# Eight heads at a step in an RWKV recurrence, and SBUF tiles on 64-byte boundaries

## The chip, the cores and the metric

The kernel runs on one core of one Trainium2 chip. The metric is the device time of one execution in microseconds. Three runs of the kernel before took 2035.17 to 2036.27, median 2035.74.

## The reference, cut to what matters

Two transformer blocks are computed on 512 positions of width 1024, all in float32. The first block mixes three branches (a short convolution, a stick-breaking attention, an RWKV-7 recurrence), then has cross attention and a convolutional feed-forward net (FFN); the second has two attentions (FoX and NSA) and a squared-ReLU MLP. The change is in the recurrence, which has eight heads with a 64x64 state each:

```
def step(state, inp):
    r_t, w_t, k_t, v_t, kk_t, a_t = inp
    sa = einsum("bhvk,bhk->bhv", state, kk_t)
    state = state * w_t - sa x (kk_t * a_t) + v_t x k_t
    return state, einsum("bhvk,bhk->bhv", state, r_t)
out = scan(step, 0, ...)                       # 512 steps
out = ((out - mean) * rsqrt(var + GN_EPS)) * lnx_w + lnx_b
return (out + bonus) * sigmoid(xg) @ g_lora
```

## The kernel before, in words

Every large product is made of three matmuls in the type float32r (high by high, low by high, high by low: lines 161, 162, 163 in `mm3`), with 128x128 weights and, mostly, 512 streamed columns. Weights come from HBM in pieces of 4 KB a partition (`wpiece`): SP issues the load, ScalarE rounds the high part (line 145), VectorE or, while `lpool` is set, GpSimd subtracts the low part (line 146). The pieces rotate through two buffers of a base pool and, in some stages, one or two of an extra pool that `weights` opens (two buffers and one extra in the FFN, two and two in the last MLP). These three lines are called the gemm matmuls below.

The recurrence works on chunks of 64 positions: 8 chunks, in two halves of four. `rwkv_prep1` makes, per chunk and head, the decayed keys and queries (tiles `rkr` with kap and rho, `rKB`) and their products `rAB` (line 869); `rwkv_prep2` inverts the triangular part of `rAB` with many matmuls of 16x16 and 32x32 (lines 924 to 945). `rwkv_scan` then goes from chunk to chunk, in two copies with four heads each (`scan(0)`, `scan(1)`):

- line 992: kap (64 weight columns) against the state, for a pair of heads; line 993: a head's `rAB` against the values `rvu`, on top of it, in PSUM partitions 64 to 127; VectorE copies the sum to `rrhs` (line 995);
- line 998: the inverted block against `rrhs`; VectorE copies it into `rvu` (line 999);
- line 1003: the state's update; line 1009: rho (64 weight columns) against the old state; line 1010: `rAB` against `rvu`, added to it in the bank `o`; VectorE adds the update to the decayed state (lines 988, 1016);
- `turn` transposes the next chunk's values and keys on TensorE (lines 969, 974), and after every second chunk `rwkv_post` normalises 128 positions (line 1034 is its matmul).

float32 matmuls run as two passes, each a row of the trace; transposes as one.

All of this is filler work beside gemm matmuls: `first_mixer` weaves `rwkv_mix` with `fill()` (the projections of the recurrence, the convolution branch, the gates, the attention's queries). The order on each engine is then set when the program is built: a scheduler with a model of the engines places the recurrence's instructions between the gemm matmuls, and at run time each engine keeps to that order and waits where it must.

Of the kernel before, what the change touches and what calls it, by code (L numbers as in the profile page):

```python
# [16 lines left out]
T = 512  # L17
# [53 lines left out]

class Core:


    def __init__(self, tc, ctx, cst):
        self.tc, self.nc, self.ctx = tc, tc.nc, ctx
        nc = self.nc
        self.const = ctx.enter_context(tc.tile_pool(name="const", bufs=1))
        self.xp = ctx.enter_context(tc.tile_pool(name="xn", bufs=1))
# [3 lines left out]
        self.wp = ctx.enter_context(tc.tile_pool(name="w", bufs=2))  # L83
# [663 lines left out]
def rwkv_project(core, pool, tmp, w, xh, xl, P, mid, pieces):  # L747

    nc = core.nc
    kr = pool.tile([128, 2, 4, T], F32, name="rkr")  # L750
    R = {"k": kr[:, 0], "r": kr[:, 1], "kr": kr, "v": pool.tile([128, 4, T], F32, name="rv")}
# [4 lines left out]
    def shift(dst, j, ps):  # L756
        t = tmp.tile([128, T + 1], F32, name="ff", bufs=3)
        nc.gpsimd.memset(t[:, 0:1], 0.0)
        nc.scalar.activation(t[:, 1:T + 1], ps, AF.Identity, scale=P["mu"][:, j:j + 1])
        nc.vector.scalar_tensor_tensor(dst, ps, P["omu"][:, j:j + 1], t[:, 0:T], op0=ALU.mult, op1=ALU.add)  # L760
# [15 lines left out]
def rwkv_prep1(core, pool, tmp, P, hf, wait):  # L776
# [6 lines left out]
    rp, kp = (R[n][:, :, ts] for n in "rk")  # L783
    KR = R["kr"][:, :, :, ts]

# [39 lines left out]
    for j in range(4):  # L825
        nc.scalar.activation(sq[:, j], kp[:, j], AF.Square, scale=col("k_k", j))
# [22 lines left out]
    tt(k2, k2, kp, op=ALU.mult)  # L849
    for j in range(4):  # L850
        nc.vector.scalar_tensor_tensor(kp[:, j], kp[:, j], col("k_k", j), pss[j // 2][:, j % 2 * 256:j % 2 * 256 + 256], op0=ALU.mult, op1=ALU.mult)
    KB = pool.tile([128, 4, 4, 2, CH], F32, name="rKB", bufs=2)
    tt(a, kp, a, op=ALU.mult)
# [3 lines left out]
    tt(ct(kp), ct(kp), E[:, :, :, 0:CH], op=ALU.mult)  # L857
    for j in range(4):
        nc.vector.scalar_tensor_tensor(k2[:, j], rp[:, j], col("r_k", j), k2[:, j], op0=ALU.mult, op1=ALU.mult)
    tt(ct(rp), ct(rp), E[:, :, :, 1:], op=ALU.mult)  # L860
# [3 lines left out]
    for c in range(4):  # L864
        for par in range(2):
            hp = slice(64 * par, 64 * par + 64)
            ps = core.pbank().rearrange("p (j t) -> p j t", j=4)
            for j in range(4):
                mm(ps[:, j], KB[hp, j, c].rearrange("p a t -> p (a t)"), KR[hp, :, j, c * CH:(c + 1) * CH], start=True, stop=True)  # L869
# [81 lines left out]
def rwkv_scan(core, pool, P, hf, g, S, o, y):  # L951
# [5 lines left out]
    js = slice(2 * g, 2 * g + 2)  # L957
    KB, AB, wc, bon = core.half[hf]
    KB, AB, wc, bon = KB[:, js], AB[:, :, :, js], wc[:, js], bon[:, :, 4 * g:4 * g + 4]
    KR = core.R["kr"][:, :, js, hf * 256:hf * 256 + 256]  # L960
    vp = core.R["v"][:, js, hf * 256:hf * 256 + 256]
    vb = None
    heads = [(j, par, slice((2 * j + par) * 64, (2 * j + par) * 64 + 64), slice(64 * par, 64 * par + 64)) for j in range(2) for par in range(2)]
    def turn(c):

        vu = pool.tile([128, 256], F32, name="rvu", bufs=4)
        ps = core.sbank()
        for j in range(2):
            nc.tensor.transpose(ps[0:64, j * 128:j * 128 + 128], vp[:, j, c * CH:c * CH + CH], core.ident)
        nc.scalar.activation(vu[0:64], ps[0:64, 0:256], AF.Copy)  # L970
        kw = pool.tile([128, 2, 128], F32, name="rkw", bufs=2)
        tt(kw, KB[:, :, c].rearrange("p j a t -> p j (a t)"), wc[:, :, c].to_broadcast([128, 2, 128]), op=ALU.mult)
        for j in range(2):
            nc.tensor.transpose(ps[:, 256 + j * 128:384 + j * 128], kw[:, j], core.ident)
        kt = pool.tile([128, 2, 128], F32, name="rkt", bufs=4)
        nc.scalar.activation(kt.rearrange("p j t -> p (j t)"), ps[:, 256:512], AF.Copy)
# [4 lines left out]
    for c in range(4):  # L981
        first = hf == 0 and c == 0
        vu, kt = ahead
        if not first:
            sw = pool.tile([128, 2, 64], F32, name="rsw", bufs=2)
            for par in range(2):
                hp = slice(64 * par, 64 * par + 64)
                tt(sw[hp], S[hp, :, hp], wc[hp, :, c].to_broadcast([64, 2, 64]), op=ALU.mult)
        ps = core.sbank()
# [6 lines left out]
        yield  # L996
        for j, par, h, hp in heads:
            mm(ps[64:128, 256 + h.start:256 + h.stop], AB[64:128, c, par, j, 0:64], rhs[64:128, h], start=True, stop=True)
        nc.vector.tensor_copy(vu[64:128], ps[64:128, 256:512])
        yield  # L1000
        ps = core.sbank()[:, 0:128].rearrange("p (j v) -> p j v", j=2)
        for j, par, h, hp in heads:
            mm(ps[hp, j], kt[:, j, hp], vu[:, h], start=True, stop=True)
        if c % 2 == 0:
            vb = pool.tile([128, 4, 64], F32, name="rvb", bufs=2)
        op = slice(64 * (c % 2), 64 * (c % 2) + 64)
        for j, par, h, hp in heads:
            if not first and par == 0:
                mm(o[op, j * 128:j * 128 + 128], KR[:, 1, j, c * CH:(c + 1) * CH], S[:, j], start=True, stop=False)
            mm(o[op, h], AB[:, c, par, j, 64:128], vu[:, h], start=first, stop=first or par == 1)  # L1010
        for par in range(2):
            hp = slice(64 * par, 64 * par + 64)
            if first:
                nc.vector.tensor_copy(S[hp, :, hp], ps[hp])
            else:
                tt(S[hp, :, hp], ps[hp], sw[hp], op=ALU.add)
        tt(vb[op], vu[0:64].rearrange("p (h v) -> p h v", h=4), bon[:, c].to_broadcast([64, 4, 64]), op=ALU.mult)
        if c < 3:
            ahead = turn(c + 1)
        if c % 2 == 1:  # L1020
            rwkv_post(core, pool, P, hf * 2 + c // 2, g, o, vb, y)
# [3 lines left out]
def rwkv_post(core, pool, P, t, g, ps, vb, y):  # L1025
# [3 lines left out]
    gs = slice(g * 256, g * 256 + 256)  # L1029
    o = pool.tile([128, 4, 64], F32, name="ro", bufs=1)  # L1030
    of = o.rearrange("p h v -> p (h v)")
    nc.scalar.activation(of, ps, AF.Copy)
    gt = core.sbank()[:, 0:256]
    nc.tensor.matmul(gt, core.R["g"][:, t * 128:t * 128 + 128], P["gl"][:, gs], start=True, stop=True)
    st = core.small.tile([128, 4, 1], F32, name="gst")
    nc.vector.tensor_reduce(st.rearrange("p h o -> p (h o)"), o, axis=AX.X, op=ALU.add)
    nc.vector.tensor_scalar(st, st, scalar1=1.0 / 64, scalar2=None, op0=ALU.mult)
    tt(o, o, st.to_broadcast([128, 4, 64]), op=ALU.subtract)
    sq = pool.tile([128, 256], F32, name="rkw", bufs=2).rearrange("p (h v) -> p h v", h=4)
    nc.scalar.activation(sq, o, AF.Square)  # L1040
    vr = core.small.tile([128, 4, 1], F32, name="gvr")
    nc.vector.tensor_reduce(vr.rearrange("p h o -> p (h o)"), sq, axis=AX.X, op=ALU.add)
    nc.gpsimd.tensor_scalar(vr, vr, scalar1=1.0 / 64, scalar2=GN_EPS, op0=ALU.mult, op1=ALU.add)
    rs = core.small.tile([128, 4, 1], F32, name="grs")
    nc.gpsimd.tensor_tensor(rs.rearrange("p h o -> p (h o)"), vr.rearrange("p h o -> p (h o)"), core.mhalf[:, 0:4], op=ALU.pow)
# [744 lines left out]
```

## Time and profile before

| | |
|---|---|
| profiled execution | 2035.63 us, span 2033.7 us |
| median of three runs | 2035.74 us |
| mean granted TensorE clock | 0.983 of full speed |
| TensorE (PE) busy | 1971.8 us, 97%, 10908 matmul rows |
| VectorE / ScalarE / GpSimd busy | 1142.3 / 845.2 / 319.9 us |
| gemm matmuls, recurrence between them | about 110 to 432 us from the span's start |

The page's busy time of PE is a sum of pipelined matmuls, so it can't tell how quickly they follow on each other. That is read from the timeline: the difference between the starts of one row and of a later one, divided by the matmuls between.

### The profile page before, as it was taken

The numbers are of one execution on the slowest core, as the hardware profiler recorded it, in microseconds if no ns is written. First come the engines' busy times: TensorE is split into PE (matmuls) and PEld (weight loads), VectorE is DVE, ScalarE is ACT, GpSimd is POOL, SyncE is SP. The second block draws the span as 40 slices with busy tenths as digits, with TensorE's granted clock in tenths as the row PEclk, the third lists the DMA queues.
The fourth block names the chain that finished last, engine by engine and source line by source line (L and its number), as shares of the span: only waits on it lengthen the run. The fifth ranks groups of instructions, "written<-read, shape, count | busy, mean of one in ns | idle before, by whom it ended". The sixth has DMA issues, their size and how long they took to land.

```text
span 2033.7 us, 28099 instructions
## 1 busy us (share of the span) xinstructions
PE 1971.8 (97%) x10908; PEld 1645.9 (81%) x10908; DVE 1142.3 (56%) x1933; ACT 845.2 (42%) x1478; POOL 319.9 (16%) x375
## 2 busy tenths in 40 slices
PE   6999999999899999999999998999999999999998
PEld 5777777778878888788888887888888878888886
DVE  3458453426877545555364456666789754344343
ACT  4433222225644444344243346557766433232232
POOL 1333123334330100200000003002243120000000
PEclk9999989999999999999999998999999999999999
DMA  5223223233347551322333335543222632333331
GB/s 169 73 68 80 68 71 102 90 118 94 105 135 239 152 162 61 105 83 83 104 96 100 94 93 166 143 126 93 63 68 89 196 114 83 101 96 94 95 102 52
DMA packets 281304, 215.03 MB, mean 106 GB/s; under 512 B 28270, under 2 KB 240900, under 8 KB 281044
## 3 DMA queue, kind: packets, MB, share of 16 engines
q1 hardware_dynamic: 261364, 205.23, 33.5%
q10 hardware_dynamic: 19808, 8.02, 1.6%
q8 instruction: 86, 1.41, 0.3%
q14 instruction: 46, 0.38, 0.1%
HBM read 195.35 MB, written 20.48 MB: 106 GB/s over the span
## 4 chain that ended last, share of the span: by engine, by line
PE 85%; DVE 7%; ACT 3%; issue 2%; DMA 2%; POOL 1%; SPq 1%; ACTq 0%; DVEq 0%; POOLq 0%
PE g L161 16%; PE g L162 16%; PE g L163 16%; PE s L161 9%; PE s L163 9%; PE s L162 9%; PE s L589 1%; PE s L603 1%; PE s L285 1%; PE p L869 1%; DVE sbr L673 1%; PE s L577 1%; PE s L576 1%; DMA wr<-in_ca_wkv_dram 1%; DVE ptl L153 1%
## 5 line engine op out<-in xcount | busy, mean ns | idle before, releaser
L145 ACT ACTIVATE wh<-wr 128x1024 fp32r<-128x1024 f32 x307 | 323.6, 1056 | 602.5 <-PE g L162 193.5
L146 DVE TENSOR_TENSOR wl<-wr,wh 128x1024 fp32r<-128x1024 f32 (+1 forms) x240 | 295.2, 1232 | 422.0 <-ACT wh L145 418.1
L161 PE MATMUL g<-xh,wh 128*128 128x512 f32 (+1 forms) x1168 | 454.0, 390 | 6.2 <-DVE rkr L760 2.4
L162 PE MATMUL g<-xl,wh 128*128 128x512 f32 (+1 forms) x1168 | 451.8, 387 | 2.1 <-DVE xl L153 2.1
L163 PE MATMUL g<-xh,wl 128*128 128x512 f32 (+1 forms) x1168 | 451.3, 387 | 0.0
L161 PEld LDWEIGHTS g<-xh,wh 128*128 128x128 f32 x1168 | 224.4, 193 | 50.4 <-issue 3.6
L162 PEld LDWEIGHTS g<-xl,wh 128*128 128x128 f32 x1168 | 224.7, 193 | 43.5 <-DVE xl L153 2.8
L163 PEld LDWEIGHTS g<-xh,wl 128*128 128x128 f32 x1168 | 224.2, 192 | 43.2 <-issue 1.2
L146 POOL TENSOR_TENSOR wl<-wr,wh 128x1024 fp32r<-128x1024 f32 x67 | 166.1, 2482 | 437.3 <-ACT wh L145 424.8
L161 PE MATMUL s<-wh,ah 128*128 128x512 f32 x324 | 127.1, 393 | 0.0
L163 PE MATMUL s<-wh,al 128*128 128x512 f32 x324 | 127.0, 392 | 0.0
L162 PE MATMUL s<-wl,ah 128*128 128x512 f32 x324 | 126.5, 391 | 0.0
L161 PE MATMUL s<-xh,wh 128*128 128x512 f32 x288 | 112.7, 391 | 0.0
L163 PE MATMUL s<-xh,wl 128*128 128x512 f32 x288 | 112.6, 391 | 0.0
L162 PE MATMUL s<-xl,wh 128*128 128x512 f32 x288 | 112.5, 391 | 0.0
L260 POOL TENSOR_TENSOR ss<-rss 128x1 f32<-128x1 f32 (+1 forms) x20 | 6.5, 327 | 464.4 <-ACT rsq L252 464.4
L1097 POOL TENSOR_SCALAR sy<-sy,rsm,ngate 128x128 f32<-128x128 f32 (+1 forms) x64 | 42.4, 666 | 198.8 <-DVE rsm L1095 182.8
L153 DVE TENSOR_TENSOR ptl<-s,pth 128x256 fp32r<-128x256 f32 (+3 forms) x144 | 66.8, 476 | 11.8 <-ACT pth L152 10.8
L163 PEld LDWEIGHTS s<-wh,al 128*128 128x128 f32 x324 | 60.8, 188 | 13.9
L162 PEld LDWEIGHTS s<-wl,ah 128*128 128x128 f32 x324 | 60.8, 188 | 13.6
L161 PEld LDWEIGHTS s<-wh,ah 128*128 128x128 f32 x324 | 60.8, 188 | 13.1
L1093 ACT ACTIVATE sy<-sy,m 128x128 f32<-128x128 f32 (+1 forms) x96 | 53.6, 559 | 39.1 <-DVE m L1091 36.9
(491 smaller groups left out, 3754.4 us busy)
## 6 DMA issues: line engine op xcount, KB each, us to landing
wr<-in_w_ff_dram SPq DMA_DIRECT2D x64, 512.0 KB
wr<-in_w_comb_dram SPq DMA_DIRECT2D x62, 512.0 KB
wr<-in_ffn_up_dram SPq DMA_DIRECT2D x44, 512.0 KB
wr<-in_w_in_dram SPq DMA_DIRECT2D x36, 512.0 KB
wr<-in_ffn_down_dram SPq DMA_DIRECT2D x22, 512.0 KB
wr<-in_ca_wkv_dram SPq DMA_DIRECT2D x16, 512.0 KB
d_gate<-ff SPq DMA_DIRECT2D x24, 256.0 KB
gi<-d_gate SPq DMA_DIRECT2D x24, 256.0 KB
```

The lines of the kernel that those rows point to most:

```text
L145: self.nc.scalar.activation(h, raw, AF.Copy)
L146: (self.nc.gpsimd if pool or self.lpool else self.nc.vector).tensor_tensor(l, raw, h.bitcast(F32), op=ALU.subtract)
L153: nc.vector.tensor_tensor(l, src, h.bitcast(F32), op=ALU.subtract)
L161: mm(out, lh, rh, start=first, stop=False)
L162: mm(out, lh, rl, start=False, stop=False)
L163: mm(out, ll, rh, start=False, stop=last)
L285: nc.tensor.transpose(ps[:, j * 128:(j + 1) * 128], x[:, j * 128:(j + 1) * 128], self.ident)
L576: mm(s, q[:, qs], kk[0][:, 0:n], start=True, stop=False)
L577: mm(s, q[:, qs], kk[1][:, 0:n], start=False, stop=last)
L589: core.nc.tensor.transpose(ps[:, c], p[:, c], core.ident)
L1093: nc.scalar.activation(y, y, AF.Exp, scale=-1.0, bias=m, accum_out=sm)
L1097: nc.gpsimd.tensor_scalar(y, y, scalar1=rs, scalar2=fac, op0=ALU.mult, op1=ALU.mult)
```

## The change: what it does

1. `rwkv_scan` runs once for all eight heads instead of twice for four. `rkr` is stored chunk by chunk with kap and rho side by side, so that one matmul with 128 weight columns (new line 1019) gives for a pair of heads what lines 992 and 1009 gave; both halves stay in the bank `o`, kap's in partitions 0 to 63, rho's in 64 to 127, and the products of lines 993 and 1010 (now 1021 and 1034) are added on top. The two copies from PSUM (now `halves`) are split between VectorE and ScalarE, 256 columns each. `o` goes to SBUF by ScalarE after every chunk. `rvu`, `rkt`, `rkw`, `rsw` and `rrhs` are twice as wide, with half as many buffers or fewer. `rwkv_post` runs four times on 512 columns instead of eight times on 256, and its result leaves in 4 DMAs instead of 8, still on ScalarE's queue.
2. `Lines` rounds the size of each tile up to 64 bytes a partition (the small ones excepted), and a tile of 32 bytes at the edge of the right-hand side shifts what lies there.

```diff
+class Lines:
+    def tile(self, shape, dtype, name, **kw):
+        n, line = math.prod(shape[1:]), 64 // mybir.dt.size(dtype)
+        if n % line == 0:
+            return self.p.tile(shape, dtype, name=name, **kw)
+        t = self.p.tile([shape[0], n + -n % line], dtype, name=name, **kw)[:, 0:n]
...
+        ctx.enter_context(tc.tile_pool(name="edge", bufs=1, side="right")).tile([128, 8], F32, name="edge")
...
-            yield p
+            yield Lines(p)
...
-    kr = pool.tile([128, 2, 4, T], F32, name="rkr")
+    kr = pool.tile([128, 4, T // CH, 2, CH], F32, name="rkr")
...
+    def halves(dst, src):
+        nc.vector.tensor_copy(dst[:, 0:256], src[:, 0:256])
+        nc.scalar.activation(dst[:, 256:512], src[:, 256:512], AF.Copy)
...
+        ps = core.ps.tile([128, 512], F32, name="o")
         if not first:
...
+            for j in range(4):
+                mm(ps[:, j * 128:j * 128 + 128], KR[:, j, c].rearrange("p a t -> p (a t)"), S[:, j], start=j == 0, stop=False, skip_group_check=True)
+        for n, (j, par, h, hp) in enumerate(heads):
+            mm(ps[0:64, h], AB[0:64, c, par, j, 0:64], vu[0:64, h], start=first and n == 0, stop=n == 7, skip_group_check=True)
...
-            if not first and par == 0:
-                mm(ps[64:128, j * 128:j * 128 + 128], KR[:, 0, j, c * CH:(c + 1) * CH], S[:, j], start=True, stop=False)
-            mm(ps[64:128, h], AB[0:64, c, par, j, 0:64], vu[0:64, h], start=first, stop=first or par == 1)
-        rhs = pool.tile([128, 256], F32, name="rrhs", bufs=2)
-        nc.vector.tensor_copy(rhs[64:128], ps[64:128, 0:256])
+        rhs = pool.tile([128, 512], F32, name="rrhs")
+        halves(rhs[64:128], ps[0:64])
...
-            if not first and par == 0:
-                mm(o[op, j * 128:j * 128 + 128], KR[:, 1, j, c * CH:(c + 1) * CH], S[:, j], start=True, stop=False)
-            mm(o[op, h], AB[:, c, par, j, 64:128], vu[:, h], start=first, stop=first or par == 1)
+        for n, (j, par, h, hp) in enumerate(heads):
+            mm(ps[64:128, h], AB[:, c, par, j, 64:128], vu[:, h], start=first and n == 0, stop=n == 7, skip_group_check=True)
...
+        nc.scalar.activation(o[op].rearrange("p h v -> p (h v)"), ps[64:128], AF.Copy)
...
-    return abreast(prep1(), prep2(), scan(0), scan(1))
+    return abreast(prep1(), prep2(), scan())
```

TensorE's order, one chunk step of the recurrence. Before, where both groups of heads come together between gemm matmuls (g<-xh,wh and so on; rS is the state):

```order
L162 MATMUL g<-xl,wh 128x512
L992 MATMUL s<-rS,rkr 64x128
L993 MATMUL s<-rvu,rAB 64x64 x2
L992 MATMUL s<-rS,rkr 64x128
L993 MATMUL s<-rvu,rAB 64x64 x2
L992 MATMUL s<-rS,rkr 64x128
L993 MATMUL s<-rvu,rAB 64x64 x2
L992 MATMUL s<-rS,rkr 64x128
L993 MATMUL s<-rvu,rAB 64x64 x2
L163 MATMUL g<-xh,wl 128x512
```

The same step on TensorE after the change (the gemm lines are now 180 to 182); the next step of the chunk, line 1027, stands 21 gemm matmuls further on, and line 1032 another 19 behind that:

```order
L182 MATMUL g<-xh,wl 128x512
L180 MATMUL g<-xh,wh 128x512
L1019 MATMUL o<-rS,rkr 128x128 x4
L1021 MATMUL o<-rvu,rAB 64x64 x8
L181 MATMUL g<-xl,wh 128x512
```

Four matmuls with 64 weight columns, each between matmuls of another tile shape, have become four with 128 in a row. TensorE at the end of a chunk, after the change (line 1009 is gone from it):

```order
L180 MATMUL g<-xh,wh 128x512
L1032 MATMUL s<-rvu,rkt 64x64 x8
L1034 MATMUL o<-rvu,rAB 64x64 x8
L996 MATMUL s<-ident,rv 64x128 x4
L1002 MATMUL s<-ident,rkw 128x128 x4
L181 MATMUL g<-xl,wh 128x512
```

What stood in two places, one for each four heads, stands in one. In all, the order before has 53 places at which a gemm matmul is followed by one with weights smaller than 128x128, the order after 41, and beyond the recurrence the engines' orders are almost the same.

The tiles' first bytes, as the built programs place them (remainder after division by 256; "pool" is that of the weight pieces):

| tile | before | after |
|---|---|---|
| xh, xl; base pool wh, wl | 32 | 64 |
| extra pool of the FFN | 160 | 128 |
| extra pools of the FoX branch and the last MLP | 224 | 192 |
| fh, fl (FoX branch) | 160 | 192 |
| pth, nv (NSA attention) | 64 | 0 |
| ah, al of the last MLP | 224 | 192 |

While a matmul streams its columns, the weights of the next are loaded. For pairs of 512-column float32r matmuls, the distance between the two starts (first byte of the streamed columns less that of the next weights, modulo 256) is in the two programs:

| distance | 0 | 64 | 128 | 192 | 32 or 224 |
|---|---|---|---|---|---|
| before | 4041 | 1356 | 719 | 28 | 80 |
| after | 4087 | 74 | 1429 | 654 | 0 |

## Rows read from the trace of the kernel before

**Rows 1.** The page, busy time by engine, and the chain that ended last:

```profile
PE 1971.8 (97%) x10908; PEld 1645.9 (81%) x10908; DVE 1142.3 (56%) x1933; ACT 845.2 (42%) x1478; POOL 319.9 (16%) x375
...
PE 85%; DVE 7%; ACT 3%; issue 2%; DMA 2%; POOL 1%; SPq 1%; ACTq 0%; DVEq 0%; POOLq 0%
```

**Rows 2.** Waits of PE, window 100 to 440 us (all of them):

```profile
PE p L924 <- ACT ff L1482: 3.7, 1, 3.7
PE s L992 <- DVE rvu L999: 2.3, 1, 2.3
```

**Rows 3.** Windows: stretch, length, busy of PE, PEld, DVE, ACT, POOL, PEclk:

```profile
275.00:293.00 18.00, 15.71 (x184) 12.41 (x185) 10.91 (x20) 1.94 (x4) 4.34 (x4) 0.53 0.26 75
```

**Rows 4.** Timeline of PE, lines 992 and 993: start, length, instruction, passes:

```profile
340.53 0.39 PE L162 MATMUL g<-xl,wh 128*128 128x512 f32 x1
340.85 0.43 PE L992 MATMUL s<-rS,rkr 128*64 128x128 f32 x2
341.21 0.44 PE L993 MATMUL s<-rvu,rAB 64*64 64x64 f32 x4
...
343.78 0.50 PE L163 MATMUL g<-xh,wl 128*128 128x512 f32 x1
```

**Rows 5.** Timeline of PE, line 1009 between others, and alone:

```profile
356.05 0.39 PE L1009 MATMUL o<-rS,rkr 128*64 128x128 f32 x2
356.27 0.39 PE L1010 MATMUL o<-rvu,rAB 128*64 128x64 f32 x4
...
358.85 0.43 PE L1009 MATMUL o<-rS,rkr 128*64 128x128 f32 x2
359.22 0.44 PE L974 MATMUL s<-ident,rkw 128*128 128x128 f32 x2
```

**Rows 6.** Timeline of PE, float32 passes with 128x128 weights and 128 columns:

```profile
92.08 1.95 PE L843 MATMUL p<-ident,re 128*128 128x128 f32 x16
93.78 0.48 PE L163 MATMUL g<-xh,wl 128*128 128x512 f32 x1
```

**Rows 7.** Timeline of PE in the FFN, first matmuls of three weight pieces:

```profile
881.67 0.39 PE L161 MATMUL g<-xh,wh 128*128 128x512 f32 x1
...
887.11 0.40 PE L161 MATMUL g<-xh,wh 128*128 128x512 f32 x1
...
892.70 0.39 PE L161 MATMUL s<-xh,wh 128*128 128x512 f32 x1
```

**Rows 8.** Timeline of PE, sixteen 64x64 passes in a row:

```profile
348.54 1.14 PE L998 MATMUL s<-rrhs,rAB 64*64 64x64 f32 x16
349.61 0.50 PE L162 MATMUL g<-xl,wh 128*128 128x512 f32 x1
```

**Rows 9.** Timeline of PE in the last MLP, extra-pool pieces, 18 matmuls apart:

```profile
1698.33 0.39 PE L161 MATMUL g<-xh,wh 128*128 128x512 f32 x1
...
1702.45 0.39 PE L161 MATMUL g<-xh,wh 128*128 128x512 f32 x1
```

**Rows 10.** Timeline of PE in the FoX branch, extra-pool pieces, 18 matmuls apart:

```profile
1612.34 0.39 PE L161 MATMUL s<-fh,wh 128*128 128x512 f32 x1
...
1616.54 0.39 PE L161 MATMUL g<-fh,wh 128*128 128x512 f32 x1
```

**Rows 11.** Timeline of PE, line 603 in NSA, then in FoX:

```profile
1413.91 0.28 PE L603 MATMUL s<-pth,nv 128*128 128x256 f32 x1
1414.03 0.28 PE L603 MATMUL s<-ptl,nv 128*128 128x256 f32 x1
...
1605.37 0.28 PE L603 MATMUL s<-ptl,v 128*128 128x256 f32 x1
1605.49 0.28 PE L603 MATMUL s<-pth,v 128*128 128x256 f32 x1
```

**Rows 12.** Groups: VectorE's copy of line 995 (by source), ScalarE's rounding (page):

```profile
L995 DVE COPY rrhs<-s x16: 427/427/428, 132.5 to 416.9; 64x256 f32<-64x256 f32 x16
...
L145 ACT ACTIVATE wh<-wr 128x1024 fp32r<-128x1024 f32 x307 | 323.6, 1056 | 602.5 <-PE g L162 193.5
```

More of the change, by code (lines that the diff above doesn't have):

```diff
@@ L749, in rwkv_project @@
     nc = core.nc
-    kr = pool.tile([128, 2, 4, T], F32, name="rkr")
-    R = {"k": kr[:, 0], "r": kr[:, 1], "kr": kr, "v": pool.tile([128, 4, T], F32, name="rv")}
+    kr = pool.tile([128, 4, T // CH, 2, CH], F32, name="rkr")
+    R = {"k": kr[:, :, :, 0], "r": kr[:, :, :, 1], "kr": kr, "v": pool.tile([128, 4, T], F32, name="rv")}
     R["wa"] = pool.tile([128, T], F32, name="rwa")
@@ L759, in shift @@
         nc.scalar.activation(t[:, 1:T + 1], ps, AF.Identity, scale=P["mu"][:, j:j + 1])
-        nc.vector.scalar_tensor_tensor(dst, ps, P["omu"][:, j:j + 1], t[:, 0:T], op0=ALU.mult, op1=ALU.add)
+        x, y = ps, t[:, 0:T]
+        if len(dst.shape) == 3:
+            x, y = (v.rearrange("p (c t) -> p c t", t=CH) for v in (x, y))
+        nc.vector.scalar_tensor_tensor(dst, x, P["omu"][:, j:j + 1], y, op0=ALU.mult, op1=ALU.add)
     def ev_lora(m, ps):
@@ L782, in rwkv_prep1 @@
     ts = slice(hf * 256, hf * 256 + 256)
-    rp, kp = (R[n][:, :, ts] for n in "rk")
-    KR = R["kr"][:, :, :, ts]
+    rp, kp = (R[n][:, :, hf * 4:hf * 4 + 4] for n in "rk")
+    KR = R["kr"][:, :, hf * 4:hf * 4 + 4]
     def e():
@@ L948, in rwkv_prep2, with rwkv_scan @@
     yield
-def rwkv_scan(core, pool, P, hf, g, S, o, y):
+def rwkv_scan(core, pool, P, hf, S, y):
     nc = core.nc
@@ L999, in rwkv_scan @@
[L999 to L1007, printed above, removed]
-            if not first and par == 0:
-                mm(o[op, j * 128:j * 128 + 128], KR[:, 1, j, c * CH:(c + 1) * CH], S[:, j], start=True, stop=False)
-            mm(o[op, h], AB[:, c, par, j, 64:128], vu[:, h], start=first, stop=first or par == 1)
+            mm(pc[hp, j], kt[:, j, hp], vu[:, h], start=True, stop=True)
@@ L1013, in rwkv_scan @@
             if first:
[L1014 removed]
+                nc.vector.tensor_copy(S[hp, :, hp], pc[hp])
             else:
[L1016 to L1017 removed]
+                tt(S[hp, :, hp], pc[hp], sw[hp], op=ALU.add)
+        op = slice(64 * (c % 2), 64 * (c % 2) + 64)
+        if c % 2 == 0:
+            vb = pool.tile([128, 8, 64], F32, name="rvb")
+            o = pool.tile([128, 8, 64], F32, name="ro")
+        nc.scalar.activation(o[op].rearrange("p h v -> p (h v)"), ps[64:128], AF.Copy)
+        tt(vb[op], vu[0:64].rearrange("p (h v) -> p h v", h=8), bon[:, c].to_broadcast([64, 8, 64]), op=ALU.mult)
         if c < 3:
@@ L1020, in rwkv_scan, with rwkv_post @@
         if c % 2 == 1:
-            rwkv_post(core, pool, P, hf * 2 + c // 2, g, o, vb, y)
+            rwkv_post(core, pool, P, hf * 2 + c // 2, o, vb, y)
         yield
-def rwkv_post(core, pool, P, t, g, ps, vb, y):
+def rwkv_post(core, pool, P, t, o, vb, y):
     nc = core.nc
     tt = nc.vector.tensor_tensor
-    gs = slice(g * 256, g * 256 + 256)
-    o = pool.tile([128, 4, 64], F32, name="ro", bufs=1)
     of = o.rearrange("p h v -> p (h v)")
[L1032 to L1035, printed above, removed]
+    gt = core.sbank()
+    nc.tensor.matmul(gt, core.R["g"][:, t * 128:t * 128 + 128], P["gl"], start=True, stop=True)
+    st = core.small.tile([128, 8, 1], F32, name="gst")
@@ L1036, in rwkv_post @@
     nc.vector.tensor_reduce(st.rearrange("p h o -> p (h o)"), o, axis=AX.X, op=ALU.add)
     nc.vector.tensor_scalar(st, st, scalar1=1.0 / 64, scalar2=None, op0=ALU.mult)
-    tt(o, o, st.to_broadcast([128, 4, 64]), op=ALU.subtract)
-    sq = pool.tile([128, 256], F32, name="rkw", bufs=2).rearrange("p (h v) -> p h v", h=4)
+    tt(o, o, st.to_broadcast([128, 8, 64]), op=ALU.subtract)
+    sq = pool.tile([128, 4, 128], F32, name="rkw").rearrange("p j (a v) -> p (j a) v", a=2)
     nc.scalar.activation(sq, o, AF.Square)
-    vr = core.small.tile([128, 4, 1], F32, name="gvr")
+    vr = core.small.tile([128, 8, 1], F32, name="gvr")
@@ L1059, in rwkv_mix @@
     core.half = {}
-    o = core.ps.tile([128, 512], F32, name="o")
     def wait(u, done):
@@ L1073, in prep2, with scan @@
             yield from rwkv_prep2(core, tmp, P, hf)
-    def scan(g):
+    def scan():
         for hf in range(2):
@@ L1078, in scan @@
             yield from wait("v", core.ready)
-            yield from rwkv_scan(core, pool, P, hf, g, S[:, 2 * g:2 * g + 2], o[:, 256 * g:256 * g + 256], y)
-    return abreast(prep1(), prep2(), scan(0), scan(1))
+            yield from rwkv_scan(core, pool, P, hf, S, y)
+    return abreast(prep1(), prep2(), scan())
 def soft(core, pool, s, bias, fac=None):
```

84 lines of the change are left out of this document (46 added, 38 removed).

## The prediction

> **What bounds the kernel.** I read the page first: busy times, then the chain of waits. TensorE is busy for 97% of the span and holds 85% of the chain; every other engine, weight loads apart, is below 60% [rows 1]. So what counts is the time that TensorE's instructions take one behind the other, and the times at which it has none it may start. The waits of TensorE over the whole stage of the recurrence, 100 to 440 us, come next: there are two, 6.0 us in all [rows 2]. [...] The rest of the stage is the pitch of matmuls, and for that I went to the timeline and subtracted starts. A reader should see that the recurrence's own latency is hidden: its steps stand far apart in TensorE's order, and the gemm matmuls fill the space. A shorter chain of steps is thus worth nothing by itself. What is worth something is fewer or cheaper instructions on TensorE.
>
> **First part: the recurrence on TensorE.** Seven of the eight chunks have a state to multiply. For each of these the first step of both groups takes, from the first pass of line 992 to the next gemm matmul, 343.78 - 340.85 = 2.93 us [rows 4]: eight passes of line 992 and sixteen of line 993. Line 992 alone takes 0.36 us for two passes, because every second one is followed by another tile shape. Line 1009 adds 0.22 us for two passes where it stands between passes of line 1010, 0.37 us where it stands alone [rows 5]; there are four such pairs a chunk, at least 0.88 us. That is 3.81 us a chunk.
>
> In its place come eight passes of line 1019, with 128x128 weights and 128 columns. No row shows that form in this place; the nearest are the sixteen passes of line 843, of the same shapes, at 1.70 us, 0.106 each [rows 6]. So 0.85 us, then a change of tile shape, for which I take what a gemm matmul pays when a smaller one follows, 0.32 instead of 0.23 us [rows 4, 7], so 0.09; then sixteen passes of line 1021 in a row, as line 998 has them: 1.07 us [rows 8]. Sum 2.01 us. **Saved: 1.80 us a chunk, 12.6 us in seven.** From below: if line 1019 keeps line 992's 0.18 us a pass, 2.51 us instead of 2.01, 9.1 us are saved. From above: if all of line 1009's pairs cost 0.37 us, 16.8 us.
>
> The order has 12 places fewer at which a gemm matmul is followed by smaller weights. Each costs 0.09 us going in, and about as much coming out: sixteen passes in 1.07 us hold one exit, and at half the pitch of line 843, 0.053 us, they would take 0.85. I take 0.09 for it too. **Saved: 12 x 0.18 = 2.2 us**, between 0 and that. So the first part is worth 14.8 us, between 9 and 19.
>
> Edits with one answer: transposes keep their number of passes, line 1034 goes from sixteen passes of 256 columns to eight of 512, and the new layout of `rkr` changes no count; nothing. VectorE has 98 instructions fewer, some of them half as long, ScalarE gets 16 copies of 256 columns and 8 of `o`, and its queue issues 4 DMAs fewer: all beside TensorE, which has 19 to 21 gemm matmuls to run between two steps of the chunk. If that cover is gone, each step costs a copy; see the last rival.
>
> **Second part: where tiles begin.** The padding removes no instruction. But in the FFN three pieces of weights follow each other with the same instructions, 24 matmuls each. From 881.67 to 887.11 us, with weights of the base pool, a matmul takes 5.44 / 24 = 0.2267 us; from 887.11 to 892.70, with those of the extra pool, 5.59 / 24 = 0.2329 us [rows 7]. What differs is where the weights begin: in the base pool at the same remainder by 256 as xh, in the extra pool 128 bytes from it. At distance 64 the pitch is 4.12 / 18 = 0.2289 us [rows 9], at 192 it is 4.20 / 18 = 0.2333 [rows 10]. For 32 and 224 I take the price of 128. With the table of distances, what is paid over 0.2267 us is before 1356 x 0.0022 + 719 x 0.0062 + 28 x 0.0066 + 80 x 0.0062 = 8.1 us, after 74 x 0.0022 + 1429 x 0.0062 + 654 x 0.0066 = 13.3 us. **Cost: 5.2 us.** Bounds: 5.2 if the prices carry over; a gain of 8.1 if on 64-byte boundaries no distance costs anything.
>
> [...]
>
> Does the 64-byte boundary itself quicken a matmul? Line 603 streams 256 columns in NSA from tiles on such a boundary, in FoX from tiles 32 bytes off one, each time at distance 0: 0.12 us from start to start in both [rows 11]. I take nothing.
>
> **Clock and waits.** The low stretch [rows 3] falls on the bursts of 16x16 matmuls of the inversion, with a wait of 2.3 us on the recurrence's copy [rows 2] and many small passes among them. The 15.7 busy us at 0.53 would take about 8.3 at full clock, so up to 7 us are there to win, and as much to lose if another such stretch comes. The bursts stay, but they stand farther apart in the new order. I take a gain of 2 us, between -7 and +7.
>
> **Sum.** -14.8 + 5.2 - 2 = -11.6 us on the profiled execution's 2035.63 us, which is 0.1 under the median: **2024.0 us**.
>
> **The rivals.**
>
> 1. [...] Chance 0.25.
>
> 2. The boundary quickens all gemm matmuls. [...] Against it: the pitches of [rows 11]. Chance 0.04.
>
> 3. Nothing to be measured. Line 1019 at 0.18 us a pass (9.1 us saved), no gain from the places, 5.2 us paid for distances, and a little more at the low clock: about 2033 us. Chance 0.08.
>
> 4. Slower: one chain instead of two. TensorE keeps to its order, so a step that isn't ready holds up all gemm matmuls behind it. Two groups gave the scheduler other steps to put in between; now every step waits for VectorE and for ScalarE, behind whatever these run. A copy takes 0.43 us, a rounding on ScalarE 1.06 us [rows 12], and the cover is 19 gemm matmuls, 4.3 us. A chunk has three such steps, 24 in all. The point at which it decides is 11.6 / 24 = 0.5 us of wait a step, or a copy that is ready 4.8 us after its matmuls. If one step in each chunk waited as line 992 did once, 2.3 us [rows 2], 8 x 2.3 = 18.4 us would come: 2042 us. For it: that wait was on just such a copy. Against it: one wait in all of the stage, and cover of several times copy and rounding together. Chance 0.08.
>
> The forecast has what is left, 0.55, with a range of its own from 2015 to 2032.
>
> **Range and chances.** A difference within 0.2%, 4.1 us, is about what a measurement of this kernel can't tell from no change. Faster by more: the forecast and rivals 1 and 2, 0.84; within: rival 3, 0.08; slower: rival 4, 0.08. From 2006 (rival 1 with the upper bound of the first part and no distance paid) to 2033 (rival 3) holds all but rivals 2 and 4.
>
> **What would show it.** Line 1019 in the timeline at about 0.11 us a pass and the next gemm matmul some 2.0 us behind its first; no wait of TensorE over 3 us between 240 and 420 us; the FFN's extra-pool pieces still near 0.233 us a matmul, the MLP's extra-pool pieces up from 0.229 to 0.233, base-pool pieces at 0.2267. [...] The prediction is wrong if the time is not within the range, or if it comes out right while the pitch of the MLP's pieces hasn't moved.

## The result, and the profile after

The changed kernel took 2013.24 us (median of 4 runs, 2010.61 to 2016.94), the kernel before in the same job 2036.01 us: ratio 0.9887, 95% interval 0.9865 to 0.9908, a gain of 22.8 us. A second job (label e5_again below) gave 2015.52 against 2034.56 us, 0.9905 (0.9893 to 0.9917), 19.0 us. The profiled executions differ by 2035.63 - 2016.94 = 18.7 us. The forecast was 2024.0, a gain of 11.6. The sign and the range (2006 to 2033) were right, but the gain came out larger by 7 to 11 us. Of the two times, 2013.24 lies below the forecast's own narrower range (2015 to 2032) and 2015.52 at its edge; both lie in what would come if distances cost nothing after the change (rival 1: 2035.6 - 14.8 - 2 = 2018.8, and down to 2010.7 without the 8.1 us paid before). So the time alone doesn't tell the forecast from that rival. The pitches below do.

The page after, busy time of PE and the other engines, and the shares of the chain that ended last:

```profile
PE 1958.1 (97%) x10844; PEld 1642.5 (82%) x10844; DVE 1115.8 (55%) x1835; ACT 850.8 (42%) x1474; POOL 321.5 (16%) x367
...
PE 88%; DVE 6%; ACT 2%; issue 2%; POOL 1%; DMA 1%; SPq 1%; ACTq 0%; DVEq 0%; POOLq 0%
```

TensorE is still the bound [rows 1], with 97% busy and 88% of the chain. It has 64 passes fewer: 56 of line 1009 and 8 of the normalisation's matmul. Busy time tells little of the rest, since it sums pipelined matmuls.

Waits of PE after, window 100 to 440 us (all of them):

```profile
PE p L865 <- DVE re L858: 3.7, 1, 3.7
```

The two waits of before [rows 2] are gone; one of 3.7 us, on the preparation's VectorE work and not on a copy of the recurrence, is new. It comes at 167 us, ahead of the 240 to 420 us in which the prediction wanted none, and there is none there. The windows of 275 to 293 us and of the whole stage after, then of the whole stage before (columns as in [rows 3], with DMA share and GB/s behind them):

```profile
275.00:293.00 18.00, 18.00 (x308) 15.44 (x305) 8.63 (x12) 5.90 (x10) 4.71 (x2) 0.89 0.35 105
...
100.00:421.20 321.20, 317.42 (x2530) 260.22 (x2529) 155.15 (x245) 100.84 (x159) 106.58 (x50) 0.96 0.31 88
100.00:443.70 343.70, 337.70 (x2596) 264.98 (x2595) 181.99 (x344) 95.53 (x163) 106.37 (x56) 0.96 0.29 81
```

The stretch that was at 0.53 [rows 3] is at 0.89, but others fell in its place: over the whole stage the granted clock is 0.96, as it was before.

Where the time went is read by comparing the starts of the same matmul in both traces. The timeline of PE after, at the matmuls of [rows 7], [rows 10] and [rows 9]:

```profile
859.01 0.39 PE L180 MATMUL g<-xh,wh 128*128 128x512 f32 x1
...
864.45 0.40 PE L180 MATMUL g<-xh,wh 128*128 128x512 f32 x1
...
870.04 0.39 PE L180 MATMUL s<-xh,wh 128*128 128x512 f32 x1
...
1589.16 0.40 PE L180 MATMUL s<-fh,wh 128*128 128x512 f32 x1
...
1676.85 0.40 PE L180 MATMUL g<-xh,wh 128*128 128x512 f32 x1
...
1681.04 0.39 PE L180 MATMUL g<-xh,wh 128*128 128x512 f32 x1
```

| the same matmul | before | after | difference |
|---|---|---|---|
| 1200th gemm matmul, end of the recurrence | 443.71 | 421.16 | -22.6 |
| FFN, first of the base-pool piece | 881.67 | 859.01 | -22.7 |
| FoX branch | 1612.34 | 1589.16 | -23.2 |
| last MLP, first of an extra-pool piece | 1698.33 | 1676.85 | -21.5 |
| end of the span | 2033.7 | 2015.1 | -18.6 |

The gain is made in the recurrence's stage, but for 0.9 us that the two traces differ by already at the 100th gemm matmul (37.57 and 36.70 us); 4.6 us are given back from the FoX branch on, where the extra pools lie 128 bytes from xh instead of 64. The pitches in the rows above are 5.44 / 24 = 0.2267 us in the base pool, 5.59 / 24 = 0.2329 in the FFN's extra pool, 4.19 / 18 = 0.2328 in the MLP's (0.2289 before [rows 9]).

One chunk's first step in the timeline after, to hold against [rows 4]:

```profile
338.94 1.05 PE L1019 MATMUL o<-rS,rkr 128*128 128x128 f32 x8
339.93 1.14 PE L1021 MATMUL o<-rvu,rAB 64*64 64x64 f32 x16
341.00 0.50 PE L181 MATMUL g<-xl,wh 128*128 128x512 f32 x1
341.33 0.39 PE L182 MATMUL g<-xh,wl 128*128 128x512 f32 x1
```

From line 1019's first pass to the next gemm matmul are 2.06 us; 2.01 were worked out. The first gemm matmul behind the block takes 0.33 us to the start of the next, not 0.23; more on this below.

### The profile page after: what moved, and what is told of

Same layout as the page of the kernel before. It is cut to its first block, busy times and chain, and to the rows that moved or that the text cites. A ratio compares the mean times of both kernels' runs of the same rounds, so it can differ in the third digit from the quotient of the medians.

```text
span 2015.1 us, 27841 instructions
## 1 busy us (share of the span) xinstructions
PE 1958.1 (97%) x10844; PEld 1642.5 (82%) x10844; DVE 1115.8 (55%) x1835; ACT 850.8 (42%) x1474; POOL 321.5 (16%) x367
## 4 chain that ended last, share of the span: by engine, by line
PE 88%; DVE 6%; ACT 2%; issue 2%; POOL 1%; DMA 1%; SPq 1%; ACTq 0%; DVEq 0%; POOLq 0%
PE g L180 17%; PE g L181 16%; PE g L182 16%; PE s L180 9%; PE s L182 9%; PE s L181 9%; PE s L608 1%; PE s L622 1%; PE s L304 1%; PE p L891 1%; DVE sbr L692 1%; PE s L596 1%; PE s L595 1%; DVE ptl L172 1%; DMA wr<-in_ca_wkv_dram 1%
## 5 line engine op out<-in xcount | busy, mean ns | idle before, releaser
L172 DVE TENSOR_TENSOR ptl<-s,pth 128x256 fp32r<-128x256 f32 (+3 forms) x144 | 66.7, 475 | 12.1 <-ACT pth L171 11.2
```

Source lines behind the costliest of these rows:

```text
L172: nc.vector.tensor_tensor(l, src, h.bitcast(F32), op=ALU.subtract)
```

## The experiments

Every ratio is to the kernel before, run in the same job; before took 2034.77 us beside the first four, 2034.56 beside the second four, 2032.53 and 2034.26 beside the last ones. Sums "by starts" add, for all records of a line up to the recurrence's end, the time from a row's start to the start of the next row on TensorE; for lines 992 and 1009 together that is 18.7 us before, for line 1019 after 7.2. These sums hold some rows at the lower clock level (a granted clock of 0.50, in windows of before from 276 to 292 us and of after from 293 to 302; at the upper level it is 1.00, from 250 to 270 us before). So a second one is given, "the stage at full clock": all starts on TensorE from the 100th to the 1200th gemm matmul, with rows at the lower level counted at their kind's mean at the upper one (a kind is a line of the recurrence, or the gemm matmuls with another line just before, just behind or on neither side), and waits over 0.2 us left out. It is 385.6 us before, 364.8 us in the changed kernel and 365.1 in its second trace (e5_again).

### One half of the change alone

The recurrence without the padding:

```diff
 class Lines:
-        if n % line == 0:
+        if True:
...
-        ctx.enter_context(tc.tile_pool(name="edge", bufs=1, side="right")).tile([128, 8], F32, name="edge")
```

> The change's recurrence without its padding: every tile begins where it did before. Theory A (the change's trace: 22.5 us gained up to 445 us by the recurrence, 4.4 us given back in the last MLP, whose extra-pool pieces went from distance 64 to 128): the price of the layout goes, 2013.2 - 4.4 = 2008.8 us, MLP extra-pool pieces at 0.229 us a matmul again. Rival B (part of the unforeseen gain comes from the 64-byte boundaries in the recurrence's stage): slower than the change, 2016 to 2022 us.

Measured: 2009.56 us, 0.9880 (0.9865 to 0.9895). The MLP's extra-pool piece is back at (1674.86 - 1670.74) / 18 = 0.2289 us a matmul. Rows of its timeline, 18 matmuls apart:

```profile
1670.74 0.39 PE L179 MATMUL g<-xh,wh 128*128 128x512 f32 x1
...
1674.86 0.39 PE L179 MATMUL g<-xh,wh 128*128 128x512 f32 x1
```

It isn't slower than the change, so rival B falls. That it is faster is not shown by the times, whose intervals overlap; the pitch shows it for the MLP. Its stage at full clock is 365.1 us, the changed kernel's.

The padding without the recurrence (`Lines` and the tile at the edge put into the kernel before):

> The padding alone, with the recurrence of before. Theory A: 2036.0 + 4.4 = 2040.4 us (5.2 by the table of distances: 2041.2), up to 445 us the same as before. Rival B: faster than before, 2029 us or so, with the gain ahead of 445 us.

Measured: 2038.93 us, 1.0018 (1.0009 to 1.0027), so 1.8 to 5.5 us slower. Its waits of PE, 100 to 445 us, are on the lines of the old recurrence [rows 2] (942 and 1010 are lines 924 and 992 of before):

```profile
PE p L942 <- DVE ry L940: 3.3, 1, 3.3
PE s L1010 <- DVE rvu L1017: 2.1, 1, 2.1
```

Theory A holds: the padding alone costs about 4 us, and all the gain is the recurrence's. The stage at full clock is 385.6 us, as before the change.

### Taking the recurrence apart

One chain over eight heads, but kap and rho multiplied apart, in the alternation of before:

```diff
-            for j in range(4):
-                mm(ps[:, j * 128:j * 128 + 128], KR[:, j, c].rearrange("p a t -> p (a t)"), S[:, j], start=j == 0, stop=False, skip_group_check=True)
-        for n, (j, par, h, hp) in enumerate(heads):
-            mm(ps[0:64, h], AB[0:64, c, par, j, 0:64], vu[0:64, h], start=first and n == 0, stop=n == 7, skip_group_check=True)
+        for j, par, h, hp in heads:
+            if not first and par == 0:
+                mm(ps[0:64, j * 128:j * 128 + 128], KR[:, j, c, 0], S[:, j], start=True, stop=False)
+            mm(ps[0:64, h], AB[0:64, c, par, j, 0:64], vu[0:64, h], start=first, stop=first or par == 1)
...
+                mm(ps[64:128, j * 128:j * 128 + 128], KR[:, j, c, 1], S[:, j], start=True, stop=False)
```

> The change with kap and rho taken apart again, in the pattern of before: a pair's kap (64 weight columns) followed by its two products with rAB in the first step, rho in the same way in the third; one chain over eight heads, the split copies and the padding stay. Theory A: the starts in the change's trace give 11.6 us to the merged product (lines 992 and 1009 took 18.8 us, line 1019 takes 7.2) and some 3 us to the longer runs of one tile shape on lines 1021 and 1034; these come back, 2013.2 + 14 = 2027 us, and the rest, about 8 us, is from one chain instead of two. Rival C (the single chain gives nearly all: fewer places between the gemm matmuls, fewer waits): 2013 to 2017 us.

Measured: 2025.42 us, 0.9960 (0.9947 to 0.9972). On the padded layout the single chain gives 1.0018 - 0.9960 = 0.58% (12 us), the rest of the change in the recurrence 0.55 to 0.73% (11 to 15 us, from the change's two ratios in other jobs). The stage at full clock divides it more sharply: 385.6 us become 377.7 with the single chain, 7.9 us, and 364.8 with the rest, 12.9 us. Neither the merged product nor the chain has nearly all, so rival C falls. Its timeline, one first step:

```profile
346.81 0.43 PE L1020 MATMUL o<-rS,rkr 128*64 128x128 f32 x2
347.17 0.44 PE L1021 MATMUL o<-rvu,rAB 64*64 64x64 f32 x4
347.54 0.43 PE L1020 MATMUL o<-rS,rkr 128*64 128x128 f32 x2
347.90 0.44 PE L1021 MATMUL o<-rvu,rAB 64*64 64x64 f32 x4
...
349.74 0.50 PE L181 MATMUL g<-xl,wh 128*128 128x512 f32 x1
```

Two passes take 0.36 us and four take 0.37, the same as in [rows 4], where two chains ran.

Then line 1019 as two matmuls of 64 weight columns, four for kap and four for rho, with nothing between them:

```diff
-                mm(ps[:, j * 128:j * 128 + 128], KR[:, j, c].rearrange("p a t -> p (a t)"), S[:, j], ...
+                mm(ps[0:64, j * 128:j * 128 + 128], KR[:, j, c, 0], S[:, j], ...
+            for j in range(4):
+                mm(ps[64:128, j * 128:j * 128 + 128], KR[:, j, c, 1], S[:, j], ...
```

> The change with line 1019 as two matmuls of 64 weight columns each, four for kap and four for rho, all eight in a row; nothing else. 56 passes more. Theory D (a pass costs by its 128 streamed columns, not by its weights): 56 x 0.11 to 0.13 = 6 to 7 us more, 2020 us. Rival E (half the weight columns, half the time, so what cost before was the alternation of tile shapes): 2013 to 2015 us.

Measured: 2013.20 us, 0.9892 (0.9879 to 0.9906): the change's time, with 56 passes more. That is rival E's time, but its reason isn't shown: by starts the two lines take 4.8 + 6.4 = 11.2 us where line 1019 took 7.2. The timeline holds both prices (L1019 is kap, L1021 rho):

```profile
358.80 0.76 PE L1019 MATMUL o<-rS,rkr 128*64 128x128 f32 x5
359.29 0.32 PE L1021 MATMUL o<-rS,rkr 128*64 128x128 f32 x1
359.39 0.27 PE L1019 MATMUL o<-rS,rkr 128*64 128x128 f32 x1
359.45 0.27 PE L1021 MATMUL o<-rS,rkr 128*64 128x128 f32 x1
...
359.67 0.71 PE L1021 MATMUL o<-rS,rkr 128*64 128x128 f32 x5
360.31 1.14 PE L1023 MATMUL o<-rvu,rAB 64*64 64x64 f32 x16
```

Passes of one half alone start 0.109 us apart (median), hardly less than passes with 128 weight columns in a run (0.112). Where kap and rho alternate they start 0.055 us apart. (The 0.49 us from kap's first start to rho's first are not five such distances: rho's pass starts 0.007 us behind kap's fifth. The 0.098 us of the expectation below divide by five.) That asked for a run of its own, kap and rho of a pair of heads behind each other:

```diff
             for j in range(4):
-                mm(ps[0:64, j * 128:j * 128 + 128], KR[:, j, c, 0], S[:, j], ...
-            for j in range(4):
-                mm(ps[64:128, j * 128:j * 128 + 128], KR[:, j, c, 1], S[:, j], ...
+                for a, op in enumerate((slice(0, 64), slice(64, 128))):
+                    mm(ps[op, j * 128:j * 128 + 128], KR[:, j, c, a], S[:, j], ...
```

> The run on line 1019 apart, with kap and rho of a pair of heads one behind the other (kap, rho, kap, rho, ...) instead of four for kap and then four for rho. In the trace of that run passes that alternate between kap (output partitions 0 to 63) and rho (64 to 127) start 0.055 us behind each other, passes of kap alone 0.098. Theory L (products with 64 weight columns that go to different halves of the partitions run side by side): the sixteen passes take about 16 x 0.055 = 0.9 us from the first start to the first product with rAB, little more than the change's eight at 0.98, and some 3 to 4 us less in all chunks than in the run on line 1019 apart; the time is that of the change, 2011 to 2015 us. Rival M (each pass has its price, 0.085 on the mean of that run): 1.36 us a chunk, as in that run.

Measured: 2013.77 us, 0.9895 (0.9877 to 0.9912). The timeline:

```profile
373.84 1.09 PE L1020 MATMUL o<-rS,rkr 128*64 128x128 f32 x16
374.87 1.14 PE L1022 MATMUL o<-rvu,rAB 64*64 64x64 f32 x16
```

Sixteen passes in 1.03 us, and by starts 7.25 us in all for 112 passes, against 7.15 for the change's 56. Within a run they start by turns 0.007 and 0.102 us apart, 0.109 a pair. Theory L holds: two products of 64 weight columns for different halves of the partitions shared the time of one. The 4 us less than in the run before are in these rows alone; the two times, 2013.20 and 2013.77 us, can't show them. So merging kap and rho is no cheaper in itself than putting them side by side; what counted is that nothing of another shape stood between (7.2 us in a run, 11.3 in the alternation of the next run).

The last piece has the merged product and the old alternation:

```diff
-            for j in range(4):
-                mm(ps[:, j * 128:j * 128 + 128], KR[:, j, c].rearrange("p a t -> p (a t)"), S[:, j], ...
         for n, (j, par, h, hp) in enumerate(heads):
+            if not first and par == 0:
+                mm(ps[:, j * 128:j * 128 + 128], KR[:, j, c].rearrange("p a t -> p (a t)"), S[:, j], ...
             mm(ps[0:64, h], AB[0:64, c, par, j, 0:64], vu[0:64, h], ...
```

> The change with the same matmuls in another order: in the first step of a chunk each of line 1019's four matmuls (128x128 weights) is followed by its two products with rAB (64x64 weights), instead of four and then eight in a row. The passes stay the same in number and size; the order has 156 changes of tile shape in the recurrence's stage instead of 119. Theory J (each change of tile shape costs TensorE 0.09 us before it, and the first pass behind it is longer too): 37 changes more, from 37 x 0.091 = 3.4 us to 7.3 us if a change costs 0.2 us as between the two runs on kap and rho; 2016 to 2021 us, and the pass of line 1021 ahead of line 1019 at 0.148 us from start to start instead of 0.058. Rival K (the number of passes decides, their order doesn't): the time of the change, 2012 to 2015 us.

Measured: 2020.77 us, 0.9943 (0.9928 to 0.9959), 8 to 11 us more than the change's two ratios; between the 100th and the 1300th gemm matmul its profiled execution takes 411.4 us, that of the changed kernel in the job before 405.5. The timeline, one first step:

```profile
340.51 0.39 PE L1020 MATMUL o<-rS,rkr 128*128 128x128 f32 x2
340.82 0.44 PE L1021 MATMUL o<-rvu,rAB 64*64 64x64 f32 x4
341.20 0.49 PE L1020 MATMUL o<-rS,rkr 128*128 128x128 f32 x2
341.61 0.44 PE L1021 MATMUL o<-rvu,rAB 64*64 64x64 f32 x4
...
343.57 0.50 PE L182 MATMUL g<-xh,wl 128*128 128x512 f32 x1
```

From the first pass to the next gemm matmul: 3.06 us, with the same 24 passes that take 2.06 in the change. Theory J holds, rival K falls; the stage at full clock, 371.5 us, is 6.4 to 6.7 us over the change's two, 0.17 to 0.18 us for each of the 37 changes of shape. By starts:

| lines | before | one chain, apart, alternating | merged, alternating | apart, in runs | merged, in runs (the change) |
|---|---|---|---|---|---|
| kap and rho against the state | 18.7 | 17.9 | 11.3 | 11.2 | 7.2 |
| 993, now 1021 | 11.6 | 12.2 | 12.6 | 9.9 | 9.9 |
| changes of tile shape in the stage | 210 | 167 | 156 | 117 | 119 |
| the stage at full clock | 385.6 | 377.7 | 371.5 | 367.5 | 364.8 |

(The changes of shape are counted in the built orders, from the 100th to the 1300th gemm matmul. With kap and rho in pairs the stage at full clock is 364.3 us.)

### The copies

```diff
 def halves(dst, src):
-        nc.vector.tensor_copy(dst[:, 0:256], src[:, 0:256])
-        nc.scalar.activation(dst[:, 256:512], src[:, 256:512], AF.Copy)
+        nc.vector.tensor_copy(dst, src)
```

> The change with each of the two PSUM copies of a chunk whole on VectorE (512 columns) instead of split between VectorE and ScalarE. Theory H (the recurrence's latency lies beside gemm matmuls): no difference over 3 us from the changed kernel, no new wait of TensorE on the copies. Rival I (the single chain is near to deciding, so the split is what keeps it hidden): waits on rrhs or rvu in the trace, 5 us or more.

Measured: 2011.92 us, 0.9889 (0.9876 to 0.9901). The only wait of PE between 100 and 440 us:

```profile
PE p L865 <- DVE re L858: 3.0, 1, 3.0
```

No wait on `rrhs` or `rvu`: theory H holds, and the split hides nothing that was not hidden. The edit also changed TensorE's order, to 111 changes of tile shape instead of 119; the stage at full clock is 363.5 us, 1.3 to 1.6 under the changed kernel's two.

### The distances

The changed kernel once more, beside the next two runs:

> The changed kernel once more, as it is, beside the three runs below: 0.988 to 0.990 of the kernel before, 2011 to 2014 us.

Measured: 2015.52 us, 0.9905 (0.9893 to 0.9917), a little less gain than expected.

Distances made 0:

```diff
+PAD = {"w_ffn": 64, "w_mlp": 128, "w_out": 128, "w_out2": 128}
...
-        with self.pool(name, bufs=more) as p:
+        with self.pool(name + "_p") as q, self.pool(name, bufs=more) as p:
+            if PAD.get(name):
+                q.tile([128, PAD[name] // 4], F32, name="pad")
```

> The change with 64 or 128 bytes of padding ahead of four extra pools of weights, so that what is opened on top of them begins at the same remainder by 256 as the base pool and xh. Pairs of 512-column matmuls at distance 0: 5880 instead of 4087, at 128: 284 instead of 1429, at 192: 6 instead of 654. Theory F (the distance between streamed columns and next weights is what costs, by the prices of the trace before): 13.3 us paid become 2.0, so 11.3 us less than the changed kernel in the same job, about 2001 us; pieces of the extra pools in the FFN and the MLP at 0.227 us a matmul. Rival G (the layout's 4 us have another cause, or the pitch differs by pool for another reason): within 3 us of the changed kernel.

Measured: 1999.70 us, 0.9831 (0.9818 to 0.9843), 15.8 us under the changed kernel of that job. FFN and MLP in its timeline (24, 24 and then 18 matmuls apart):

```profile
848.51 0.39 PE L185 MATMUL g<-xh,wh 128*128 128x512 f32 x1
...
853.95 0.39 PE L185 MATMUL g<-xh,wh 128*128 128x512 f32 x1
...
859.39 0.39 PE L185 MATMUL s<-xh,wh 128*128 128x512 f32 x1
...
1660.59 0.39 PE L185 MATMUL g<-xh,wh 128*128 128x512 f32 x1
...
1664.67 0.39 PE L185 MATMUL g<-xh,wh 128*128 128x512 f32 x1
```

5.44 / 24, 5.44 / 24 and 4.08 / 18: 0.2267 us everywhere, as theory F has it. This profiled execution is the fastest of its five, and its span is 19.6 us under that of the changed kernel: 4.4 us lie ahead of the 1200th gemm matmul (starts of 415.62 against 419.99 us), 15.2 behind it. Ahead of it no distance of 512-column matmuls differs, and the stage at full clock is 365.0 us, against 365.1: what differs is the granted clock, 0.98 instead of 0.96, and 0.8 us of waits. Behind it, too, the clock stood at its lower level for less time, 29.2 us against 36.2. Why it did, was not tried. What the distances are worth at one clock is read from the last run below.

Distances made 192:

```diff
         self.wp = Lines(ctx.enter_context(tc.tile_pool(name="w", bufs=2)))
+        self.wp.tile([128, 16], F32, name="shift", bufs=1)
```

> The change with 64 bytes ahead of the base pool's tiles, which moves all that lies above it too. Pairs at distance 0: 1349 instead of 4087, at 64: 102, at 128: 669 instead of 1429, at 192: 4124 instead of 654. Theory F: 31.6 us paid instead of 13.3, 18.3 us more than the changed kernel, about 2030 us; base-pool pieces in the FFN at 0.233 us a matmul. Rival G: within 3 us of it.

Measured: 2024.01 us, 0.9949 (0.9938 to 0.9960), 8.5 us over the changed kernel, half of what was expected. The base-pool piece of the FFN:

```profile
857.25 0.39 PE L181 MATMUL g<-xh,wh 128*128 128x512 f32 x1
...
862.85 0.39 PE L181 MATMUL g<-xh,wh 128*128 128x512 f32 x1
```

5.60 / 24 = 0.2333 us: the price is there. But up to the 1200th gemm matmul, with some 1050 pairs at 192, it isn't slower (419.08 against 419.99 us). Three things oppose it: that stage's granted clock is 0.97 instead of 0.96, its waits over 0.2 us are 2.6 us shorter, and the pitch at distance 0 was not 0.2267 but 0.2280 on the mean of all pairs at full clock (longer gaps than 0.26 us left out), so that the step to 0.2333 is 5.3 ns there. At full clock the stage is longer, 369.9 us against 365.1. Behind the stage 11.4 of the 18.3 us were expected, and the traces differ by 6.4. Rival G falls; the size is explained in part.

### Both together

> The kernel of the run on distance 0 with the PSUM copies whole on VectorE, whose order has 111 changes of tile shape in the recurrence's stage instead of 119. Theory J: 8 x 0.09 = 0.7 us less than the run on distance 0, which the times can hardly tell from it; 1997 to 2001 us, faster than both kernels. Against it: VectorE has the bound of the waits on the inversion, and the copies could make these longer, 2002 us or more.

Measured: 2000.62 us, 0.9834 (0.9814 to 0.9853), not to be told from the run on distance 0. What lies behind the 1200th gemm matmul, in windows of the changed kernel (e5_again), of the run on distance 0 and of this one:

```profile
420.00:2013.70 1593.70, 1557.45 (x7915) 1314.08 (x7913) 916.84 (x1531) 702.31 (x1230) 192.73 (x277) 0.99 0.36 110
415.60:1994.10 1578.50, 1541.46 (x7915) 1309.93 (x7913) 916.10 (x1531) 701.97 (x1230) 192.85 (x277) 0.99 0.36 111
418.50:1999.30 1580.80, 1543.72 (x7915) 1312.96 (x7913) 917.81 (x1531) 701.71 (x1230) 196.82 (x277) 0.99 0.36 110
```

In this run the clock stood at its lower level there for 36.1 us, as in the changed kernel (36.2), and the stretch is 12.9 us shorter: near theory F's 11.3. The stage at full clock is 363.5 us, as in the run with whole copies alone. This run and the run on distance 0 are the fastest kernels of the study, about 34 us below the kernel before.

## Why the prediction was right, and where its sum was off

**The bound and the cover.** Right: TensorE is still the bound (97% busy), no wait on the recurrence's copies came, and the run with whole copies shows slack left (one wait, 3.0 us, on the preparation). Rival 4 did not happen.

**Lines 992, 993 and 1009.** Right. The step worked out 12.6 us; by starts the three took 18.7 + 11.6 = 30.3 us and lines 1019 and 1021 take 17.0, so 13.3, or 12.9 at full clock. The reason was only half right: the prediction counted passes, with one change of shape a group. The runs show that the order makes more of it than the number: the merged product is at 11.3 us in the alternation and at 7.2 in a run, and apart it is at 7.25 if its halves stand side by side.

**"The order has 12 places fewer ... Saved: 12 x 0.18 = 2.2 us, between 0 and that." This is the term that was mis-sized.** It counted only gemm matmuls followed by smaller weights. At full clock, from the 100th to the 1200th gemm matmul, the rows show three parts:

- TensorE paid at changes of tile shape inside the recurrence too (line 1021's last pass 0.148 us ahead of another shape, 0.058 ahead of its own), and the order has 91 fewer of them in all, 210 to 119. Lines 1010, 998 and 1003 fell from 23.8 to 21.9 us, and the transposes, costed at nothing because their passes stay the same, from 8.9 to 6.7; the normalisation's matmul rose from 2.9 to 3.3. Together 3.8 us (by starts it seems 4.8, but 1.1 of that is the lower clock level, at which rows of lines 1010, 998 and 1003 fell in the kernel before).
- Coming back cost a gemm matmul 0.11 us (0.336 instead of 0.227), and 0.09 even behind passes of its own tile shape (0.314). The places at which another line stands between gemm matmuls went from 71 to 51, not by 12.
- Going in cost the 0.09 us foretold (0.318 instead of 0.227), but only ahead of another tile shape (0.226 to 0.237 ahead of lines with 128x128 weights and of the transposes). With coming back, gemm matmuls beside other lines cost 3.2 us less.

So the term is worth about 7 us instead of 2.2, and the first part 12.9 + 7 = 19.9 us, not 14.8, a little over the upper bound of 19.

**Clock and waits, -2 us.** Its size came out near half, by other means than the prediction had. 6.0 us of waits became 3.7. The clock's part was not won: the lower level lasts 27.3 us of the stage instead of 30.7, but it falls on 56 gemm matmuls instead of 49 and costs about 13.6 us over full clock, against 12.2. Together -0.9 us. The estimate that the stretch of [rows 3] would take about half its time at full clock was wrong as well: its 16x16 passes took as long at the lower level. Two bursts of line 924 in the timeline before, the first at the upper level, the second at the lower:

```profile
271.85 1.76 PE L924 MATMUL p<-ry,rAB 16*16 16x16 f32 x64
...
283.06 1.80 PE L924 MATMUL p<-ry,rAB 16*16 16x16 f32 x61
```

From start to start these passes take 0.026 us at the upper level (a granted clock of 1.00 from 271.85 to 273.60 us) and 0.027 at the lower (0.50 from 283.06 to 284.90).

**Where tiles begin, +5.2 us.** Right: 4.6 us given back in the profiled execution, 3.7 (1.8 to 5.5) by the padding alone, at the pitches foretold for the base pool, the FFN and the MLP. That distances cost nothing after the change (rival 1) falls with 0.2328 us between aligned tiles at distance 128 and with the run at distance 0. Rival 2 falls with 0.2267 us between aligned tiles, the same as on boundaries of 32 bytes before [rows 7]. Rival 3 falls with line 1019's 7.2 us, 0.13 a pass and not 0.18, and with the time.

**The sum.** Up to the 1200th gemm matmul it is 19.9 us for the first part, 0.9 for clock and waits, 0.9 in the other rows of the stage and 0.9 ahead of it, 22.6 in all, as measured. Another 0.6 us come off up to the FoX branch and 4.6 are given back from there on, which leaves the 18.6 between the spans. The medians say more, 22.8 and 19.0. So the forecast's sum had its largest term and its cost right and one term at a third of its size; that the time still fell into the range owes something to luck, since the range was drawn down to 2006 for distances that cost nothing (rival 1), which did not happen. The changed kernel's four runs show why one pair isn't enough: two at a mean granted clock of 0.983 took 2016.94 and 2015.31 us, two at 0.987 took 2010.61 and 2011.17. The single chain's 12 us between two medians are not all in rows either: the profiled executions of the padding alone and of the single chain differ by 10.4 us, and 7.9 of them are the stage at full clock. What moves the clock was not separated.

## What to carry to other kernels

Count the changes of tile shape in TensorE's order and the places at which small work stands between large matmuls, not the passes alone, and put matmuls of one shape in a row before merging anything: the same 24 passes took 2.06 us in runs and 3.06 in alternation here. Where a stream of matmuls is the bound, tabulate the distance between the starts of the streamed operand and the weights, here modulo 256 bytes, and try to make it 0: here a matmul took 0.2267 us at 0 and 0.2333 at 192. Being on a 64-byte boundary was worth nothing by itself (0.2267 us at distance 0 on 32 and on 64 bytes). Padding that aligns every tile can move the ones that matter apart, as it did the MLP's (from 64 to 128, 0.2289 to 0.2328 us): tabulate the pairs, not the addresses.

## What the runs showed of the hardware

- A change of tile shape cost TensorE 0.09 us before it: the last pass of line 1021 starts 0.148 us ahead of a row of another shape and 0.058 ahead of its own kind, a gemm matmul 0.318 instead of 0.227. Ahead of other lines with 128x128 weights it takes 0.226 to 0.236 us, and ahead of the transposes of values no more either (0.227 to 0.237, lines 996 after and 969 before), though these have 64 weight columns. The first pass behind a change can be longer as well: line 1019's second pass starts 0.112 us behind the first in a run, 0.213 in the alternation (medians).
- The first gemm matmul behind a block of other lines takes 0.336 us to the next, and 0.314 where the block's last pass had 128x128 weights too. So coming back had a price without a change of tile shape. What it is paid for was not tried.
- Matmuls with 64 weight columns ran side by side where they went to different halves of the partitions: 0.109 us for a pair (kap and rho in pairs), and 0.109 for each pass in the same half (kap and rho apart, in runs).
- 16x16 passes took the same time at a granted clock of 0.5 as at 1.0 (0.027 and 0.026 us); gemm matmuls between gemm matmuls took 0.43 instead of 0.23.
- The load of the next weights ran beside the matmul ahead of it: in the trace after, line 180's matmul starts at 859.01 us and lasts 0.39, and the load for line 181 starts at 859.01 and lasts 0.19. With the distance of the two starts taken modulo 256, the pitch of 512-column float32r matmuls was 0.2267 us at 0, 0.2289 at 64, 0.2329 at 128, 0.2333 at 192. At 0, 128 and 192 it was so on boundaries of 32 and of 64 bytes alike; 64 was measured on 32 alone. That it is 256 and no other modulus, and why the distance matters, was not shown.
